# A two-layer trunk (forgetting attention, then retention) on Strassen products: the order of every engine written out in the kernel

## The chip, the cores and the metric

One core of one Trainium2 chip. The metric is device time in microseconds of one execution, the median of several. The core has TensorE (PE in the profile; its weight loads are listed apart, as PEld), VectorE (DVE), ScalarE (ACT), GpSimd (POOL) and SyncE (SP). SP issues most transfers; POOL issues those that add to what lies in memory. Each engine takes its instructions in the order of its own list, and waits on semaphores for the others.

## The reference, cut to what matters

512 tokens of width 2048, all in fp32, two layers. Every layer is one branch and one normalisation:

```python
h = layer_norm(DEEPNORM_ALPHA * h + branch(h, ...), ln_gain[i], ln_bias[i])
# layer 0, fox_branch: q, k, v, gate, f_logit = split(h @ w_in);  16 heads of 128
q, k = rms_norm(q, q_gain), rms_norm(k, k_gain)
c = cumsum(log_sigmoid(f_logit + b_f), axis=1)
s = q @ k.T * scale + c[:, None] - c[None, :]          # causal mask, softmax
branch = (softmax(s) @ v * silu(gate)) @ w_out
# layer 1, retention_branch: q, k of 8 heads of 256, v and gate of 8 heads of 512
q, k = rotary(q), rotary(k) * 256 ** -0.5
o = (q @ k.T * decay) @ v                              # given in chunks of 128, with a carried state
branch = (group_norm_heads(o) * silu(gate)) @ w_out
```

Nearly all arithmetic is in the projections: 2048 x 8192 and 2048 x 2048 in layer 0, 2048 x 12288 and 4096 x 2048 in layer 1.

## The kernel before, in words

**Products.** A projection is cut into units (class `Unit`). A unit multiplies a 2 x 2 arrangement of quarters of the activations (rows m, columns n) by a 2 x 2 arrangement of quarters of weights with seven products, p1 to p7, where the plain way has eight. The activations are prepared in seven forms (a11, s1, a12, s2, s4, s3, a22), sums and differences of their quarters that stay on chip while a layer uses them. The weights' sums are made on DVE as they stream: `operand` (L184-203) loads a block of 512 KB with `load` (L178-182), keeps a running chain tile for p1, p5, p6, p4 (L202 adds the next quarter to it) and adds two blocks for p7 (L199). Three staging tiles (ring `st`) and four chain tiles take the loads.

**Precision.** fp32 operands are split in a high and a low part (`split`, L141-144): ACT copies the high part (L143), DVE subtracts it to get the low part (L144). `mm3` (L146-150) multiplies with three matmuls: high by high, high by low, low by high.

**Blocks.** A block is 128 partitions by 1024 weights: "wide" blocks make 12 matmuls of 512 columns, "narrow" ones 24 of 256. There are 16 narrow units of 14 blocks (q and k of Fox pairs and of retention heads) and 18 wide ones of 28 (4 of Fox values and gates, 2 of the Fox output, 8 of retention values and gates, 4 of its output): 728 blocks. Each needs one ACT copy and one DVE subtraction, and 416 need a sum on DVE as well. The results of products are combined in `after` (L242-260): ACT copies p1, p5 and p6 out of their PSUM bank (`keep`, L237-239), DVE adds later products to them (L251, L255, L258), and the unit's `sink` gets each of the four result quarters.

**Everything else** stands between blocks: per Fox pair the norms (`normed`: L478 squares, L484 scales, L491 transposes, L495 splits) and two heads (`head`: L518 adds the forget bias, L523 the row extreme, L524 exp, L526 scale, L533 transposes, L534 copies, L544 products with v, L553 gate). A head's output goes to DRAM as parts of the next forms, L354 through POOL's queue where it is added to what lies there, L356 through SP's. `fetch_form` (L358-) brings forms back. After the Fox output units 4 and 5 come `add_z` (L670-685: residual and statistics), `to_columns` and `turn` (L700-720: normalise, transpose) and `combine` (L300-322: the forms of the new layer). A retention head has rotation (L771-774), scores (L789), mixing and group norm (L818-820), transposes (L832-841); its gate waits in DRAM (L607, L816). At the end `store` (L896-907) normalises with DVE, ACT (L903) and POOL (L904).

**What sets the order.** Three things. `ahead` delays each block's multiplication by two blocks behind its preparation. `pending` is a list of side steps: `tick` runs a share of it after each block, spread evenly over the blocks left in the unit, and `finish_pending` runs all that is left at the seams between layers. Above both, the framework's scheduler reorders instructions on each engine by its own estimate of when they are ready, so a line of the kernel does not show where its instruction stands.

```python
def tick():
    blocks[0] -= 1
    for _ in range(max(1, -(-len(pending) // max(blocks[0], 1)))):
        if pending:
            pending.popleft()()
```

Of the kernel before, what the change touches and what calls it, by code (L numbers as in the profile page):

```python
# [17 lines left out]
AX = mybir.AxisListType  # L18

P = 128  # L20
D = 2048
S = 512
# [23 lines left out]
def blocks_of(n, *groups):  # L46
# [9 lines left out]
HELD = ([("p1", c) for c in range(4)] + [(p, c) for p in ("p5", "p6", "p2") for c in range(3)],  # L56
        [(p, 3) for p in ("p5", "p6", "p2")] + blocks_of(4, ("p3", "p7"), ("p4",)))
# [8 lines left out]


@with_exitstack
def trunk(ctx: ExitStack, tc: tile.TileContext, xq, x, fb_f, columns, wf_in, narrow, wide, ln_g, ln_b, rot, decay,
# [4 lines left out]
    dram = ctx.enter_context(tc.tile_pool(name="dr", bufs=1, space=bass.MemoryType.DRAM))  # L74

# [8 lines left out]

    def raw8(tag):
        return pool.tile([P, 8, 256], F32, name="raw", tag=tag)

    def mmp():
        return psum.tile([P, 512], F32, name="mmp", tag="mmp", bufs=2)

    def trp():
        return mmp().rearrange("p (a b) -> p a b", a=4)
# [4 lines left out]
    make_causal_mask(nc, causal, NEG)  # L97

# [4 lines left out]

    pending = deque()
    blocks = [0]

    def tick():
        blocks[0] -= 1
        for _ in range(max(1, -(-len(pending) // max(blocks[0], 1)))):
            if pending:  # L110
                pending.popleft()()

    def finish_pending():
        while pending:
            pending.popleft()()


    ahead = deque()

    def advance(n):  # L120
        while len(ahead) > n:
            ahead.popleft()()

    def rsqrt(dst, src, n, scale, eps):

        h = pool.tile([P, n], F32, name="rsq_h", tag=f"rsq_h{n}", bufs=2 if n < 4 else 1)
        t = pool.tile([P, n], F32, name="rsq_t", tag=f"rsq_t{n}", bufs=2 if n < 4 else 1)
# [5 lines left out]
        for _ in range(3):  # L133
            if n == 1:
                nc.vector.scalar_tensor_tensor(t, dst, dst, h, op0=ALU.mult, op1=ALU.mult)
            else:
                nc.vector.tensor_mul(t, dst, dst)
                nc.vector.tensor_mul(t, t, h)
            nc.vector.scalar_tensor_tensor(dst, t, 1.5, dst, op0=ALU.subtract, op1=ALU.mult)
# [13 lines left out]
    forms = {}  # L153

    def new_form(name):
        forms[name] = [pool.tile([P, 8, 256], F32R, name=name, tag=t) for t in HOME[name]]

    def split_form(name, src, sl):
        split(src, *(t[sl] for t in forms[name]))

    chains = [0]
    pairs_of_banks = ["b0", "b1", "b2"]

    class Unit:
# [3 lines left out]
        def __init__(self, w, n, sink, rows=True):  # L168
            self.w, self.n, self.sink, self.rows = w, n, sink, rows
# [3 lines left out]
            self.keeps = {"p1": "k0", "p5": "k1", "u2": "k2"} if self.wide else {"p1": "k1", "p5": "k2", "u2": "k0"}  # L173
            self.banks = self.both = None
            self.bank, self.kept, self.chain, self.lent = {}, {}, {}, {}
            self.left = {p: self.blocks for p in FORM}

        def load(self, q, c, tag=None):  # L178
            kw = dict(tag=tag) if tag else dict(tag="st", bufs=3)
            t = pool.tile(self.shape, F32, name="w_raw", **kw)  # L180
            nc.sync.dma_start(t.rearrange("p a b -> p (a b)"), self.w[self.n, int(q[1]) - 1, int(q[0]) - 1, c])
            return t

        def operand(self, p, c, following, streamed):  # L184

            if p in ("p1", "p5") and not streamed and c not in self.chain:
                self.chain[c] = self.load("11", c, f"q{chains[0] % 4}")
                chains[0] += 1
            if p == "p1":
                return self.load("11", c) if streamed else self.chain[c]  # L190
            if p in ("p2", "p3"):
                t = self.load({"p2": "21", "p3": "22"}[p], c)
                if following == (SHARES[p], c):
                    self.lent[following] = t
                return t
            if p == "p7":
                b = self.lent.pop((p, c), None) or self.load("22", c)
                t = self.load("12", c)
                nc.vector.tensor_add(t, t, b)  # L199
                return t  # L200
            t = self.lent.pop((p, c), None) or self.load({"p5": "12", "p6": "22", "p4": "21"}[p], c)
            nc.vector.tensor_add(self.chain[c], self.chain[c], t)  # L202
            return self.chain[c]

        def accumulator(self, b):

            if self.both is None:
                if self.banks is None:
                    self.banks = dict(zip("xzy", pairs_of_banks))
                    pairs_of_banks[:] = pairs_of_banks[1:] + pairs_of_banks[:1]  # L210
                t = psum.tile([P, 2, 512], F32, name="acc", tag=self.banks[b])
                return t if self.wide else t[:, 0].rearrange("p (e n) -> p e n", e=2)
            if b == "x":
                self.pair = psum.tile([P, 2, 512], F32, name="acc", tag=self.both)
            return self.pair[:, "xzy".index(b) > 0].rearrange("p (e n) -> p e n", e=2)

        def multiply(self, p, c, w, streamed):
            a = forms[FORM[p]]
            b = BANK[p]
            new = self.left[p] == self.blocks and p in ("p1", "p2", "p5")  # L220
            if new:
                self.bank[b] = self.accumulator(b)
            self.left[p] -= 1
            n = self.shape[1]
            for k in range(n):
                for e in range(2):
                    es = slice(e * P, (e + 1) * P)
                    if self.rows:
                        l, r = [t[:, n * c + k, es] for t in a], [t[:, k] for t in w]
                    else:  # L230
                        l, r = [t[:, k, es] for t in w], [t[:, n * c + k] for t in a]
                    mm3(self.bank[b][:, e], l, r, new and k == 0 and (e == 0 or self.wide),
                        self.left[p] == 0 and k == n - 1)
            if self.left[p] == 0:
                self.after(p, streamed)

        def keep(self, what, bank):  # L237
            self.kept[what] = t = pool.tile([P, 2, self.shape[2]], F32, name=what, tag=self.keeps[what])
            nc.scalar.activation(t, self.bank[bank], AF.Copy)
# [726 lines left out]
```

## Time and profile before

| | |
|---|---|
| Median of 3 runs | 2584.55 us (2584.49 to 2587.41) |
| Profiled execution, own time | 2578.53 us |
| Its span; mean clock granted to TensorE | 2576.8 us; 0.964 |
| DMA | 507.86 MB, 197 GB/s over the span |

The span runs from the first to the last instruction of the profiled execution; the own time also holds what lies around it. In a row of a table by stretches, each engine's busy time is followed by its number of instructions; PEclk is the share of full clock that TensorE was granted there, so busy time times PEclk is the work at full clock. In the rows of groups the columns are: line, engine, operation, what it writes and reads, how often, then busy time in all, the mean of one in ns, and the idle time ahead of it with what ended it. In the rows of waits: engine, line and tile that waits, what it waits for, us in all, times, longest.

### The profile page before, as it was taken

Reading aid. Unit: us, or ns where it says so; the run is one execution under the profiler, and the core shown is the slowest. Engines: PE = TensorE matmul, PEld = TensorE weight load, DVE = VectorE, ACT = ScalarE, POOL = GpSimd, SP = SyncE. Lnnn points to the kernel's source line nnn. Section 1 sums busy time; section 2 is a strip of 40 time slices with the busy share of each in tenths; the row PEclk is TensorE's granted clock in tenths of the full one; section 3 lists DMA queues with packets and bytes.
Section 4 is the critical chain, followed back from the end, with each engine's and each line's share of the span. In section 5 each row is a group of like instructions: output and inputs, shape, how many; then the busy total and the mean of one; then the engine's idle time right before and its main releaser. Section 6 shows DMA issues by size and latency. Waiting matters only on the chain.

```text
span 2576.8 us, 34299 instructions
## 1 busy us (share of the span) xinstructions
PE 2349.0 (91%) x12820; PEld 2001.7 (78%) x12820; DVE 2004.3 (78%) x2617; ACT 1276.9 (50%) x1891; POOL 100.8 (4%) x116
## 2 busy tenths in 40 slices
PE   6899999999997898699999999999999988897994
PEld 5788898898886687579797878788888866675773
DVE  7778687777776779887878878787878788577778
ACT  5456566666566445444454444444544444343432
POOL 0000000001101000000000000000000100100001
PEclk8999999999998999899999999999999999999997
DMA  6465746645755657467566566666676666677564
GB/s 243 156 217 168 235 150 172 217 160 159 221 190 162 217 188 269 155 196 208 178 220 194 193 191 202 181 203 189 208 212 201 190 198 216 191 241 241 193 213 147
DMA packets 213159, 507.86 MB, mean 197 GB/s; under 512 B 20080, under 2 KB 76784, under 8 KB 212736
## 3 DMA queue, kind: packets, MB, share of 16 engines
q1 hardware_dynamic: 198592, 485.22, 56.9%
q0 software_dynamic: 14400, 20.45, 5.6%
q8 instruction: 100, 1.64, 0.3%
q14 instruction: 67, 0.55, 0.1%
HBM read 430.33 MB, written 75.27 MB: 196 GB/s over the span
## 4 chain that ended last, share of the span: by engine, by line
PE 24%; DVE 14%; DMA 11%; issue 4%; ACT 4%; SPq 0%; POOL 0%; ACTq 0%; POOLq 0%; DVEq 0%
PE acc L149 7%; PE acc L150 7%; PE acc L148 7%; DVE w_l L144 5%; DMA w_raw<-in_wide 4%; ACT w_h L143 3%; DVE w_raw L202 2%; DMA w_raw<-in_narrow 2%; DMA y_s<-ny 1%; DMA cos_sin<-in_rot 1%; DMA ln_g<-in_ln_g 1%; DVE w_raw L199 1%; PE mmp L148 1%; DMA gate<-rgates 1%; DMA y_raw<-y_s 1%
## 5 line engine op out<-in xcount | busy, mean ns | idle before, releaser
L143 ACT ACTIVATE w_h<-w_raw 128x1024 fp32r<-128x1024 f32 x728 | 762.7, 1057 | 919.0 <-PE acc L150 277.0
L144 DVE TENSOR_TENSOR w_l<-w_raw,w_h 128x1024 fp32r<-128x1024 f32 x728 | 882.9, 1220 | 285.5 <-ACT w_h L143 281.1
L148 PE MATMUL acc<-w_h,s 128*128 128x512 f32 (+1 forms) x1664 | 607.7, 365 | 50.6 <-ACT w_h L143 46.6
L149 PE MATMUL acc<-w_l,s 128*128 128x512 f32 (+1 forms) x1664 | 609.2, 366 | 21.2 <-DVE w_l L144 20.4
L150 PE MATMUL acc<-w_h,s 128*128 128x512 f32 (+1 forms) x1664 | 602.6, 362 | 0.0
L148 PE MATMUL acc<-w_h,a 128*128 128x512 f32 (+1 forms) x1248 | 459.8, 369 | 47.3 <-ACT w_h L143 34.6
L149 PE MATMUL acc<-w_l,a 128*128 128x512 f32 (+1 forms) x1248 | 456.4, 366 | 33.8 <-DVE w_l L144 33.8
L150 PE MATMUL acc<-w_h,a 128*128 128x512 f32 (+1 forms) x1248 | 453.6, 363 | 0.0
L202 DVE TENSOR_TENSOR w_raw<-w_raw 128x1024 f32<-128x1024 f32 x312 | 378.5, 1218 | 69.8 <-DMA w_raw<-in_narrow 34.3
L148 PEld LDWEIGHTS acc<-w_h,s 128*128 128x128 f32 x1664 | 318.7, 192 | 108.3 <-ACT w_h L143 58.5
L149 PEld LDWEIGHTS acc<-w_l,s 128*128 128x128 f32 x1664 | 319.2, 192 | 84.2 <-DVE w_l L144 40.1
L150 PEld LDWEIGHTS acc<-w_h,s 128*128 128x128 f32 x1664 | 319.2, 192 | 43.5 <-DVE s L144 0.4
L148 PEld LDWEIGHTS acc<-w_h,a 128*128 128x128 f32 x1248 | 241.7, 194 | 91.9 <-ACT w_h L143 42.4
L149 PEld LDWEIGHTS acc<-w_l,a 128*128 128x128 f32 x1248 | 241.7, 194 | 72.4 <-DVE w_l L144 38.7
L150 PEld LDWEIGHTS acc<-w_h,a 128*128 128x128 f32 x1248 | 241.5, 194 | 35.0
L199 DVE TENSOR_TENSOR w_raw<-w_raw 128x1024 f32<-128x1024 f32 x104 | 126.9, 1220 | 51.1 <-DMA w_raw<-in_wide 39.8
L148 PE MATMUL acc<-s,w_h 128*128 128x256 f32 x512 | 145.9, 285 | 5.1 <-DVE u L255 2.0
L149 PE MATMUL acc<-s,w_h 128*128 128x256 f32 x512 | 146.1, 285 | 0.0
L150 PE MATMUL acc<-s,w_l 128*128 128x256 f32 x512 | 146.0, 285 | 0.0
L148 PE MATMUL acc<-a,w_h 128*128 128x256 f32 x384 | 110.8, 288 | 1.0 <-DVE p L258 1.0
L149 PE MATMUL acc<-a,w_h 128*128 128x256 f32 x384 | 110.1, 287 | 0.0
L150 PE MATMUL acc<-a,w_l 128*128 128x256 f32 x384 | 109.9, 286 | 0.0
(187 smaller groups left out, 2558.3 us busy)
## 6 DMA issues: line engine op xcount, KB each, us to landing
w_raw<-in_wide SPq DMA_DIRECT2D x468, 512.0 KB, 4.0
w_raw<-in_narrow SPq DMA_DIRECT2D x200, 512.0 KB, 3.6
y_raw<-y_s SPq DMA_DIRECT2D x35, 256.0 KB, 4.1
gate<-rgates SPq DMA_DIRECT2D x32, 256.0 KB, 4.6
y_s<-ny POOLq DMA_DIRECT2D x32, 256.0 KB, 7.5
y_raw<-y_a SPq DMA_DIRECT2D x26, 256.0 KB, 4.0
y_a<-y SPq DMA_DIRECT2D x24, 256.0 KB, 3.0
y_s<-y POOLq DMA_DIRECT2D x24, 256.0 KB, 7.0
```

Of the source, the lines that this page charges most:

```text
L143: nc.scalar.activation(h, src, AF.Copy)
L144: nc.vector.tensor_sub(l, src, f32(h))
L148: nc.tensor.matmul(ps, a[0], b[0], start=start, stop=False, skip_group_check=True)
L149: nc.tensor.matmul(ps, a[0], b[1], start=False, stop=False, skip_group_check=True)
L150: nc.tensor.matmul(ps, a[1], b[0], start=False, stop=stop, skip_group_check=True)
L199: nc.vector.tensor_add(t, t, b)
L202: nc.vector.tensor_add(self.chain[c], self.chain[c], t)
```

## The change

The kernel switches the framework's scheduler off (`tc.manual_schedule()`): every engine runs its instructions as the program's text issues them. A class `Order` does the ordering while the program is written. Blocks stand in one line across all units; `slot` issues what belongs to block i: results of block i - 1, sums of weights up to block i + 3, splits up to block i + 2, loads up to i + 8 as tiles come free, then the matmuls of block i, then one `step` of each waiting task. Tasks (norms, heads, fetched forms, normalisation) are generators that yield `need(...)`: the estimated DVE, ACT and PE time of their next step, slots to wait, a condition, and tiles that must be free, which `Order` counts itself. A step is passed over while DVE or ACT has a debt of over 5 us by these estimates. Where a block's form or bank isn't there, `require` makes turns without a block: all tasks go on, step by step. I call these forced turns.

```diff
+    def slot(self):
+        i, n = self.at, len(self.line)
+        self.turn()
+        self.debt = [max(0.0, d - self.time) for d in self.debt]
+        self.time = 2.8
+        if i:
+            self.finish(self.line[i - 1])
+        while self.added <= min(i + 3, n - 1):
...
+            while self.split < self.added:
+                self.split_one()
+            self.debt[0] += self.line[self.added].add()
+            self.added += 1
+        while self.split <= min(i + 2, n - 1):
+            self.split_one()
+        while self.loaded < min(i + 9, n) and all(self.free[r] >= k for r, k in self.line[self.loaded].rings().items()):
+            self.line[self.loaded].load()
+            self.loaded += 1
+        b = self.line[i]
+        self.require(b.ready)
+        b.multiply()
+        self.step()
+        self.at += 1
```

```diff
+    def require(self, met):
+        for _ in range(400):
+            if met():
+                return
+            self.turn()
+            self.debt = [max(0.0, d - 2.7) for d in self.debt]
+            self.step(True)
```

Other edits that come with it:

- Writes to DRAM move from SP's queue to POOL's: the parts of the forms (`give_forms`), values and gates, normalised rows, residuals. POOL issues 258 transfers where it issued 100; SP issues fewer.
- In the two units whose order is EARLY (the last of each layer's output), the weights' sums for p7 and p4 are made by transfers that add, 16 in all, and p4 gets a bank of its own, so that its result needs a second addition in `add_z`. The order HELD of the first Fox output unit puts p7 behind p3 block by block and one block of p2 behind both.
- Retention gates stay on chip. Statistics are finished for two row tiles at once, and half of the first normalisation runs on ACT.
- The first blocks' x is loaded and split in smaller parts. Retention's first blocks are the wide ones.
- At the end DVE does all of the normalisation; ACT's scaling and POOL's additions go.
- Heads 12 and 13 of the Fox layer go through DRAM (`late_parts`): their part of the forms s1, s2, a12, s4 and a22 is fetched while the output projection has begun.

```diff
+                nc.gpsimd.dma_start(d, self.source("22", 2 * i + c), accum_op=ALU.add)
...
-            if c % 2:
-                nc.scalar.activation(z, z, AF.Copy, scale=r)
-                nc.gpsimd.tensor_add(z, z, gb[1][:, cs])
-            else:
-                nc.vector.scalar_tensor_tensor(z, z, r, gb[1][:, cs], op0=ALU.mult, op1=ALU.add)
...
+                nc.vector.scalar_tensor_tensor(z, z, r[:, e:e + 1], gb[1][:, cs], op0=ALU.mult, op1=ALU.add)
```

Counted over the program, PE keeps its 12758 instructions; DVE goes from 2619 to 2586, ACT from 1701 to 1708. The changed order has 120 forced turns: 15 around blocks 13 to 21, 49 at the first Fox output unit (blocks 224 to 238), 34 at the second seam (blocks 260 to 301), 12 around the first retention output unit, the rest at the end; none in the stretches between.

Two places show what moves. The first is ACT at the start of the first Fox output unit, while the last heads' softmax runs: L143 is the split of weights, L518, L524, L526 and L534 the steps of heads named above. Before:

```order
L143 ACTIVATE w_h_6409<-w_raw_6407 128x1024
L524 ACTIVATE p_6333,sm_6334<-p_6333,sm_6334 128x512
L524 ACTIVATE p_6363,sm_6364<-p_6363,sm_6364 128x384
L526 ACTIVATE p_6333<-p_6333,sm_6334 128x512
L143 ACTIVATE w_h_6445<-w_raw_6442 128x1024
L526 ACTIVATE p_6363<-p_6363,sm_6364 128x384
L534 ACTIVATE pT_6388<-mmp_6389 128x4x128
L518 ACTIVATE mmp_6395<-mmp_6395,c_tok_692 128x256
L534 ACTIVATE pT_6388<-mmp_6425 128x3x128
L524 ACTIVATE p_6401,sm_6402<-p_6401,sm_6402 128x256
L143 ACTIVATE w_h_6471<-w_raw_6469 128x1024
```

And with the change, where L845 is the bias, L838 exp, L834 the scale, L828 the copies and L255 the split of forms and weights alike:

```order
L834 ACTIVATE p_8158<-p_8158,sm_8161 128x512
L838 ACTIVATE p_8169,sm_8172<-p_8169,sm_8172 128x384
L845 ACTIVATE mmp_8174<-mmp_8174,c_tok_1515 128x256
L845 ACTIVATE mmp_8174<-mmp_8174,c_tok_1515 128x128
L834 ACTIVATE p_8169<-p_8169,sm_8172 128x384
L838 ACTIVATE p_8186,sm_8189<-p_8186,sm_8189 128x256
L838 ACTIVATE p_8186,sm_8193<-p_8186,sm_8193 128x128
L828 ACTIVATE pT_8207<-mmp_8202 128x4x128
L834 ACTIVATE p_8186<-p_8186,sm_8189 128x256
L834 ACTIVATE p_8186<-p_8186,sm_8193 128x128
L255 ACTIVATE s1_7938<-y_raw_8181 128x512
L255 ACTIVATE w_h_8231<-w_q_7535 128x1024
```

Before, three to five steps of heads stand between two splits of weights. Now 28 rows of ACT stand between the splits for blocks 232 and 233, and the last of them splits what heads 12 and 13 wrote to DRAM.

The second place is DVE in retention head 1: L144 is the split, L202 the sum of weights, L818 to L820 the group norm. Before:

```order
L144 TENSOR_TENSOR w_l_12062<-w_raw_12059,w_h_12061 128x1024
L818 BN_STATS gn_st_12097<-mmp_12090 128x6
L202 TENSOR_TENSOR w_raw_12059<-w_raw_12059,w_raw_12101 128x1024
L819 BN_AGGR gn_mv_12094<-gn_st_12097 128x2
L202 TENSOR_TENSOR w_raw_12010<-w_raw_12010,w_raw_12146 128x1024
L144 TENSOR_TENSOR w_l_12105<-w_raw_12059,w_h_12104 128x1024
L820 SCALAR_TENSOR_TENSOR gate_12095<-mmp_12090,gn_mv_12094,gate_12095 128x512
L818 BN_STATS gn_st_12142<-mmp_12133 128x6
L144 TENSOR_TENSOR w_l_12150<-w_raw_12010,w_h_12149 128x1024
L819 BN_AGGR gn_mv_12094<-gn_st_12142 128x2
L202 TENSOR_TENSOR w_raw_12059<-w_raw_12059,w_raw_12197 128x1024
```

With the change L256 is the split, L447 the sum, L1324 to L1326 the group norm, and L1379 a step of the residual for the next layer:

```order
L256 TENSOR_TENSOR w_l_12069<-w_raw_11935,w_h_12068 128x1024
L447 TENSOR_TENSOR w_raw_11969<-w_raw_11969,w_raw_11935 128x1024
L1379 SCALAR_TENSOR_TENSOR z_in_11924<-ln_b_11926,z_in_11924 128x512
L256 TENSOR_TENSOR w_l_12102<-w_raw_11969,w_h_12101 128x1024
L1324 BN_STATS gn_st_12132<-mmp_12032 128x6
L1325 BN_AGGR gn_mv_12131<-gn_st_12132 128x2
L1326 SCALAR_TENSOR_TENSOR p1_11432<-mmp_12032,gn_mv_12131,p1_11432 128x512
L256 TENSOR_TENSOR w_l_12146<-w_raw_12004,w_h_12145 128x1024
L447 TENSOR_TENSOR w_raw_12073<-w_raw_12073,w_raw_12004 128x1024
L1324 BN_STATS gn_st_12178<-mmp_12136 128x6
L1325 BN_AGGR gn_mv_12131<-gn_st_12178 128x2
L1326 SCALAR_TENSOR_TENSOR p1_11432<-mmp_12136,gn_mv_12131,p1_11432 128x512
```

Now each block has its split and at most one sum, and one short step of a task behind them, always in this order.

More of the change, by code (lines that the diff above doesn't have):

```diff
@@ L184, in operand, with source @@
[L184 to L203, printed above, removed]
+        def source(self, q, c):
+            return self.w[self.n, int(q[1]) - 1, int(q[0]) - 1, c]
@@ L215, in accumulator @@
[L215 to L235, printed above, removed]
@@ L282, in run @@
[L282 to L292 removed]
+                shares = i + 1 < len(order) and order[i + 1] == (SHARES.get(p), c)
+                shared = i > 0 and order[i - 1] == ({"p7": "p3", "p4": "p2"}.get(p), c)
+                o.push(Block(self, p, c, shares, shared, streamed, then.get(i), then.get(p), before.get(i)))
```

1408 lines of the change are left out of this document (956 added, 452 removed).

## Prediction

> **What bounds the kernel now.** I read the page's busy times first, then a table of nine stretches of the span, then the pitch of single matmuls, then the waits by engine.
>
> ```profile
> span 2576.8 us, 34299 instructions
> PE 2349.0 (91%) x12820; PEld 2001.7 (78%) x12820; DVE 2004.3 (78%) x2617; ACT 1276.9 (50%) x1891; POOL 100.8 (4%) x116
> ```
>
> TensorE is the busiest, but 91% is an average, and part of it is work at a low clock. The stretches are (1) the first two units, (2) six Fox pairs, (3) the first and (4) the second Fox output unit, (5) the second normalisation with retention head 0, (6) heads 1 to 6, (7) head 7 with the first retention output unit, (8) the last three units, (9) the tail.
>
> ```profile
> core 0: us, PE busy (x) PEld busy (x) DVE busy (x) ACT busy (x) POOL busy (x), PEclk, DMA share, GB/s
> 0.00:169.00 169.00, 141.04 (x794) 121.13 (x795) 130.66 (x160) 86.11 (x127) 1.09 (x8) 0.96 0.60 208
> 169.00:787.50 618.50, 608.32 (x3913) 541.57 (x3913) 469.66 (x701) 395.38 (x793) 35.21 (x40) 1.00 0.61 185
> 787.50:908.20 120.70, 101.72 (x437) 78.43 (x436) 91.23 (x147) 67.89 (x143) 3.47 (x4) 0.90 0.65 199
> 908.20:1003.10 94.90, 86.75 (x370) 69.48 (x370) 77.03 (x107) 41.11 (x53) 0.00 (x0) 0.95 0.67 221
> 1003.10:1166.70 163.60, 135.24 (x733) 115.60 (x732) 137.46 (x166) 75.14 (x91) 0.00 (x0) 0.92 0.57 190
> 1166.70:2003.80 837.10, 799.81 (x4450) 690.62 (x4449) 668.10 (x833) 382.33 (x445) 34.78 (x40) 0.99 0.65 198
> 2003.80:2272.50 268.70, 230.49 (x1125) 190.11 (x1125) 197.31 (x248) 115.65 (x131) 13.95 (x16) 0.94 0.68 206
> 2272.50:2555.90 283.40, 245.57 (x1009) 194.77 (x1008) 218.01 (x225) 110.60 (x109) 6.07 (x4) 0.93 0.63 209
> 2555.90:2576.80 20.90, 0.01 (x1) 0.00 (x0) 14.79 (x36) 2.67 (x4) 6.24 (x4) 0.62 0.26 101
> ```
>
> PE busy times the granted clock is the work at full clock: 135.4, 608.3, 91.5, 82.4, 124.4, 791.8, 216.7, 228.4 and 0. It sums to 2279; the span holds 298 us beside it. The losses by stretch are 33.6, 10.2, 29.2, 12.5, 39.2, 45.3, 52.0, 55.0 and 20.9. So stretch 2 is nearly full, and the loss lies at the seams and in retention. DVE's share, over stretches 1 to 8, is 73 to 84%: busy, not full.
>
> What a block costs TensorE is read from the distance between matmuls, wide blocks first, then narrow:
>
> ```profile
> 1849.80 0.39 PE L149 MATMUL acc<-w_l,a 128*128 128x512 f32 x1
> ...
> 1855.92 0.39 PE L149 MATMUL acc<-w_l,a 128*128 128x512 f32 x1
> 319.73 0.28 PE L149 MATMUL acc<-w_l,a 128*128 128x256 f32 x1
> ...
> 320.93 0.28 PE L150 MATMUL acc<-w_h,a 128*128 128x256 f32 x1
> ```
>
> The first two lie 27 matmuls apart, 0.2267 us each: 12 make a wide block of 2.72 us. The others lie 10 apart, 0.12 each: 24 make a narrow block of 2.88.
>
> What TensorE waits for (us in all, times, longest), and what ACT's weight copies wait for:
>
> ```profile
> PE acc L148 <- ACT w_h L143: 81.2, 46, 8.7
> PE acc L149 <- DVE w_l L144: 54.1, 41, 15.6
> PE mmp L835 <- ACT gate L832: 21.2, 12, 4.4
> ```
> ```profile
> ACT w_h L143 <- DVE w_raw L202: 272.9, 94, 8.8
> ACT w_h L143 <- DVE w_raw L199: 155.7, 50, 9.5
> ```
>
> TensorE waits for weights that are split too late: 135 us of its waits are for their high or low half. The copy is late since the sum on DVE ahead of it was late. That is a matter of place in DVE's and ACT's orders, which the change sets, not of their rates:
>
> ```profile
> L143 ACT ACTIVATE w_h<-w_raw 128x1024 fp32r<-128x1024 f32 x728 | 762.7, 1057 | 919.0 <-PE acc L150 277.0
> L144 DVE TENSOR_TENSOR w_l<-w_raw,w_h 128x1024 fp32r<-128x1024 f32 x728 | 882.9, 1220 | 285.5 <-ACT w_h L143 281.1
> L202 DVE TENSOR_TENSOR w_raw<-w_raw 128x1024 f32<-128x1024 f32 x312 | 378.5, 1218 | 69.8 <-DMA w_raw<-in_narrow 34.3
> ```
>
> A block needs 1.22 us of DVE for the split and, in 4 of 7 products, 1.22 for a sum: at most 2.44 of 2.72, so steps of about 1 us a block fit on the average.
>
> Such waits also cost clock:
>
> ```profile
> 2543.14 0.47 PE L148 MATMUL acc<-w_h,a 128*128 128x512 f32 x1 [2.14 <-ACT w_h L143]
> ...
> 2543.91 0.57 PE L148 MATMUL acc<-w_h,a 128*128 128x512 f32 x1
> 2544.28 0.63 PE L149 MATMUL acc<-w_l,a 128*128 128x512 f32 x1
> 2544.71 0.63 PE L150 MATMUL acc<-w_h,a 128*128 128x512 f32 x1
> ...
> 2547.27 0.45 PE L150 MATMUL acc<-w_h,a 128*128 128x512 f32 x1
> ```
>
> After 2.14 us of idle the pitch is 0.43, half speed, for 3.4 us, which adds about 1.6 us. Over the stretches busy time times (1 - clock) makes 70 of the 298 us. The Trainium skill ("TensorE: Matmul & The Clock Gate", Part 1) says the gate falls to half only after an idle window of about 3.4 us. The idle row here is shorter and half speed followed, so the measurement decides. By the page's rule the short stalls left below would cost no clock, and the sum would be about 30 us lower: 5 us of clock in each of the six stretches that I leave with losses.
>
> **The change part by part.** TensorE's work is the same 12758 instructions, so 2279 us stays. What moves is where DVE and ACT work stands. Weights are summed three blocks and split two blocks ahead, always, and one short step of each task follows a block. In the steady stretches the order has no forced turn (a place where several steps run with no block between): I let the losses fall there to what fixed distances can't cover.
>
> Stretch 2: 608.3, less one pair's attention that slips behind the seam. Its small matmuls are costed from two pairs:
>
> ```profile
> 312.40:499.80 187.40, 185.63 (x1173) 163.92 (x1172) 143.39 (x217) 120.28 (x247) 6.12 (x7) 1.00 0.57 180
> ```
>
> 28 narrow and 28 wide blocks take 156.8 of 185.6, so a pair's small matmuls take 14.4; ACT has 120.3 less 56 splits of 1.057, 30.5 a pair. With 3 of loss: 608.3 - 14.4 + 3 = 597.
>
> Stretch 3 turns worse. Blocks 224 to 239 now hold the heads of two pairs, 1.8 pairs of steps, in 49 forced turns. Here ACT fills first: 16 splits make 17, 1.8 pairs at 27 (30.5 without the results kept) make 48, late forms some 13: about 78 to 80 against 16 blocks of 2.72 = 43.5. Then block 230 can't begin before heads 12 and 13 were written to DRAM and read back:
>
> ```profile
> y_raw<-y_s SPq DMA_DIRECT2D x35, 256.0 KB, 4.1
> y_s<-ny POOLq DMA_DIRECT2D x32, 256.0 KB, 7.5
> y_a<-y SPq DMA_DIRECT2D x24, 256.0 KB, 3.0
> ```
>
> A write on POOL's queue (7.5), a read on SP's (4.1), and splits behind both are 15 to 25: I take 20. With 80 + 20, twelve further blocks at 2.72 (33) and 5 for the clock, 138 against 120.7: the seam loses 17 us.
>
> Stretch 1: a lead-in, then DVE's combination of x. The first matmul now:
>
> ```profile
> 8.20 0.58 PE L148 MATMUL acc<-w_h,a 128*128 128x256 f32 x1 [8.20 <-ACT w_h L143]
> ```
>
> Loading x in smaller pieces makes that 7. Between the splits of blocks 10 and 24 DVE has 45 operations of 1.22 and small ones, 56 us, against 39.7 of PE work, less the 5.6 that splits run ahead: 11. 135.4 + 7 + 11 = 153.
>
> Stretch 4: sixteen sums in all become accumulating DMAs (two units of eight; 19.5 us of DVE). Reads are unchanged in bytes, and the DMA share of 0.67 covers them; if it didn't, 7.5 us would show once per product. 82.4 + 1 = 83; at the old loss 95.
>
> Stretch 5: 33 forced turns. Between blocks 278 and 301 DVE's instructions, at the durations of the rows above, make about 86 us against 73 for 24 blocks and the small matmuls: 13, plus 7 for the chain of normalisation and transposes and 5 of clock: 124.4 + 25 = 150.
>
> Stretches 6, 7, 8: losses fall to a third: 791.8 + 15 = 807, 216.7 + 18 = 235 (12 forced turns), 228.4 + 15 = 243. From no loss to the old one they lie between 1237 and 1389. I take the lower third because stretch 2, where the same splits run beside heavier ACT work, already loses 1.7% against 5.7, 24 and 24% of the work here: the split rate is no limit.
>
> Tail: no matmul; the rows that matter, beside POOL's work and alone:
>
> ```profile
> L906 DVE SCALAR_TENSOR_TENSOR z<-z,ln_r,ln_last 128x512 f32<-128x512 f32 x8 | 8.7, 1125 | 0.0
> L820 DVE SCALAR_TENSOR_TENSOR gate<-mmp,gn_mv,gate 128x512 f32<-128x512 f32 x32 | 23.9, 748 | 8.2 <-DMA gate<-rgates 7.8
> ```
>
> DVE takes over ACT's and POOL's part, 4 to 6 operations more, but each at about 0.75 in place of 1.125: 22 (18 to 26).
>
> Writes that stood between the weight loads on SP's queue now stand on POOL's, 258 issues for 100:
>
> ```profile
> L354 POOL DMA_DIRECT2D y_s<-ny x58 | 54.4, 1063 | 604.3 <-ACT qk_raw L467 199.5 <-DMA y_s<-ny 190.9 <-ACT ny L841 72.8
> ```
>
> At 1.06 us that is 273 us of POOL, 11% of the span, off the path except at the seam. SP gains nothing on the path while the loads run up to nine blocks ahead.
>
> Sum: 153 + 597 + 138 + 83 + 150 + 807 + 235 + 243 + 22 = 2428. The profiled execution took 2578.53 by its own time, 1.73 over its span; the median of the runs, 2584.55, is 6.02 more. So 2430 of own time, and 2436 as median.
>
> Edits with one answer, taken at nothing: the retention gates stay on chip (fewer DMAs, under shares of 0.57 to 0.68), statistics are finished for two row tiles at once, half of the first normalisation goes to ACT, which is busy 75 of 164 us in stretch 5. What hides them is TensorE's blocks; without that cover none is worth over 5 us.
>
> **The rivals.** *Leaner seams* (0.20). A forced turn may cost only its busiest engine, and the steady losses may all but vanish. For it: DVE is below 85% in every stretch. Against: 120 forced turns. Halving my 149 us of loss gives about 2365. The floor is 2279 of work, 7 of lead-in, 22 of tail and 8: 2316.
>
> *Heavier seams* (0.12). A forced turn is a round trip between engines that no block hides. One such step:
>
> ```profile
> L478 ACT ACTIVATE mmp<-qk_raw 128x128 f32<-128x128 f32 x128 | 33.8, 264 | 0.5
> L478 ACT ACTIVATION_READ_ACCUMULATOR mmp<-qk_raw 128x1 f32 x128 | 24.1, 188 | 0.0
> ```
>
> Four of each make 1.8 us; with the hand-over to the next engine I take 1.9. At that, stretch 3 holds 93 + 43.5 + 20 + 33 + 5 = 195 and stretch 5 124 + 63 = 187 and 10 for the rest: with some 15 at the start and in stretch 7, 120 us more, 2556. For it: the seam loses 29.2 us in 28 blocks already, ten times what stretch 2 loses per block.
>
> *POOL's queue* (0.05). Twelve writes of heads 12 and 13 and eight of the normalised rows stand in one line at 1.06, and two landings of 7.5 show: 36 us, 2472. The Trainium skill ("SBUF — State Buffer", Who interferes with whom) has GpSimd's DMAs starved while DVE holds the shared ports, which would make this dearer. With DVE 78% busy the L354 row still shows 1.06 us an issue; that L906 is slow beside POOL agrees with the page's lock.
>
> *Blocked in order* (0.11, slower). Each engine now waits at the head of a written order: a weight split on ACT stands behind a kept result or a step that waits for TensorE, and a scheduler no longer puts ready work first. The place is ACT's and DVE's order in the steady stretches, with some 670 blocks. It decides from 148/670 = 0.22 us a block; one DVE operation of 1.22 in every fourth block is 0.305 and 204 us: 2640. Against: splits two blocks ahead leave 5.4 us, and a step is held back once either engine owes 5 us. For: DVE's 78% leaves little to catch up with.
>
> *No change* (0.04, 2580 to 2590): the order before may already have been near this one, its losses being chains. Against: the waits for w_h and w_l come from sums that stand late.
>
> **How the numbers follow.** The forecast, 2436, has 0.48, its own range 2390 to 2490. The range over all cases is 2350 to 2590: it leaves out a quarter of the lean case, the slower rival and little else. About 0.2% is what a measurement of this kernel tells from no change. Faster: 0.48 + 0.20 + 0.05 + 0.11 of the heavier seams = 0.84; within 0.2%: 0.04; slower: the blocked order and the last 0.01, 0.12.
>
> **What would show it.** Work at full clock stays 2279. Right: stretch 6 within 800 to 820, waits of TensorE for w_h and w_l under 50 us in all, the Fox output seam longer than 120.7, with ACT the releaser, DVE's sums ahead of the copies by a block. Wrong: waits spread thinly over all steady blocks (blocked order), a seam stretch above 190 (heavier) or POOL transfers as releasers of SP's reads for more than 30 us.

## The result, and the profile after

The changed kernel takes 2813.62 us (median of four runs, 2807.18 to 2818.12) where the kernel before takes 2585.98: the ratio is 1.0873, interval 1.0843 to 1.0902. It is 8.7% slower; the forecast was 2436, 6% faster.

The first lines of the page:

```profile
span 2812.5 us, 34239 instructions
...
PE 2421.5 (86%) x12820; PEld 2044.4 (73%) x12820; DVE 2015.2 (72%) x2584; ACT 1280.6 (46%) x1898; POOL 190.8 (7%) x284
```

DVE and ACT are busy for nearly as long as before (2004.3 and 1276.9 us), so the loss is not added work of theirs. The table by stretches, cut at the same blocks as the one in the prediction:

```profile
core 0: us, PE busy (x) PEld busy (x) DVE busy (x) ACT busy (x) POOL busy (x), PEclk, DMA share, GB/s
0.00:219.40 219.40, 154.78 (x769) 132.64 (x770) 121.20 (x122) 79.25 (x111) 2.87 (x11) 0.84 0.43 150
219.40:890.70 671.30, 619.12 (x3873) 548.11 (x3872) 473.73 (x699) 378.99 (x754) 62.74 (x93) 0.97 0.53 166
890.70:1089.20 198.50, 135.47 (x503) 101.73 (x502) 101.61 (x176) 91.51 (x191) 9.21 (x12) 0.74 0.42 128
1089.20:1191.80 102.60, 83.76 (x353) 66.44 (x352) 75.43 (x102) 38.91 (x42) 9.13 (x12) 0.93 0.70 218
1191.80:1426.70 234.90, 162.63 (x746) 134.25 (x745) 132.78 (x150) 82.70 (x112) 2.14 (x4) 0.81 0.34 115
1426.70:2247.80 821.10, 795.49 (x4453) 682.08 (x4452) 681.46 (x838) 384.94 (x452) 68.78 (x101) 1.00 0.63 190
2247.80:2511.30 263.50, 230.78 (x1125) 189.47 (x1125) 201.23 (x249) 117.70 (x135) 22.45 (x31) 0.95 0.66 198
2511.30:2783.00 271.70, 239.49 (x1009) 189.67 (x1007) 202.67 (x207) 106.56 (x106) 13.43 (x20) 0.96 0.68 214
2783.00:2812.50 29.50, 0.00 (x0) 0.00 (x0) 25.07 (x48) 0.00 (x0) 0.00 (x0) 0.53 0.34 130
```

Busy time times clock is 2285 us, as before (2279). The rest is idle time of TensorE (2812.5 - 2421.5 = 391 us, before 228) and a low clock (136 us, before 70). Against before the length changes by +50, +53, +78, +8, +71, -16, -5, -12 and +9 us: lost at the two seams, at the start and in the Fox pairs, a little won in retention.

What TensorE waits for has changed in kind. Its two longest rows now are:

```profile
PE acc L260 <- ACT s L255: 92.3, 18, 12.6
PE acc L260 <- ACT w_h L255: 47.4, 12, 17.4
```

Over all such rows it waits 83.7 us for high and low parts of weights, where it waited 135.3 before, and 141.8 us for forms (tiles `s` and `a`), for which the kernel before has no row. So TensorE now stands more at forms that come late than at weights.

Two rows of the other engines show why they come late, DVE's wait for ACT's high part and ACT's for DVE's sum:

```profile
DVE w_l L256 <- ACT w_h L255: 585.1, 426, 6.6
ACT w_h L255 <- DVE w_q L451: 531.9, 225, 23.0
```

The same row of the kernel before:

```profile
DVE w_l L144 <- ACT w_h L143: 281.1, 247, 4.1
```

DVE stands 304 us longer at a low part whose high part isn't there. Such idle time costs nothing by itself; it costs where TensorE needs what stands behind it. What that looks like, two blocks of the second seam, in order of time (start, length, engine; in brackets the idle time before and what ended it):

```profile
1266.98 1.06 ACT L255 ACTIVATE w_h<-w_q 128x1024 fp32r<-128x1024 f32 x1 [5.86 <-PE acc L261]
1268.07 1.23 DVE L256 TENSOR_TENSOR w_l<-w_q,w_h 128x1024 fp32r<-128x1024 f32 x1 [5.69 <-ACT w_h L255]
1269.21 1.22 DVE L545 TENSOR_TENSOR raw<-raw 128x1024 f32<-128x1024 f32 x1
1270.46 1.06 ACT L255 ACTIVATE s<-raw 128x1024 fp32r<-128x1024 f32 x1 [2.43 <-DVE raw L545]
1271.57 0.58 PE L260 MATMUL acc<-s,w_h 128*128 128x256 f32 x1 [4.57 <-ACT s L255]
...
1277.37 0.60 ACT L339 ACTIVATE p<-acc 128x512 f32<-128x512 f32 x1 [5.85 <-PE acc L262]
1277.86 1.05 ACT L255 ACTIVATE w_h<-w_raw 128x1024 fp32r<-128x1024 f32 x1
1278.94 1.23 DVE L256 TENSOR_TENSOR w_l<-w_raw,w_h 128x1024 fp32r<-128x1024 f32 x1 [6.16 <-ACT w_h L255]
1280.08 1.22 DVE L447 TENSOR_TENSOR w_raw<-w_raw 128x1024 f32<-128x1024 f32 x1
1281.22 1.22 DVE L552 TENSOR_TENSOR raw<-raw 128x1024 f32<-128x1024 f32 x1
1282.47 1.06 ACT L255 ACTIVATE s<-raw 128x1024 fp32r<-128x1024 f32 x1 [3.56 <-DVE raw L552]
1283.58 0.58 PE L260 MATMUL acc<-s,w_h 128*128 128x256 f32 x1 [6.25 <-ACT s L255]
```

While TensorE works on the block ahead of the first excerpt, ACT stands at the copy of a weight for a later block, which waits 5.86 us until TensorE leaves one of three buffers. In the second it stands 5.85 us at L339, the copy of a result that TensorE hasn't finished, and the weight's copy stands behind that. In DVE's order come the low part of the weight, then in the second case a sum (L447), then the step (L545, L552) that makes the form which the very next block needs. So DVE and ACT idle while TensorE works, and TensorE idles (4.57 and 6.25 us) while they work.

### The profile page after: what moved, and what is told of

It is laid out like the page before. It is cut to its first block, busy times and chain, and to the rows that moved or that the text cites. A ratio compares the mean times of both kernels' runs of the same rounds, so it can differ in the third digit from the quotient of the medians.

```text
span 2812.5 us, 34239 instructions
## 1 busy us (share of the span) xinstructions
PE 2421.5 (86%) x12820; PEld 2044.4 (73%) x12820; DVE 2015.2 (72%) x2584; ACT 1280.6 (46%) x1898; POOL 190.8 (7%) x284
## 5 line engine op out<-in xcount | busy, mean ns | idle before, releaser
L255 ACT ACTIVATE w_h<-w_q 128x1024 fp32r<-128x1024 f32 x408 | 429.9, 1058 | 770.4 <-DVE w_q L451 531.9
L256 DVE TENSOR_TENSOR w_l<-w_q,w_h 128x1024 fp32r<-128x1024 f32 x408 | 497.9, 1223 | 334.7 <-ACT w_h L255 331.5
L260 PE MATMUL acc<-w_h,s 128*128 128x512 f32 (+1 forms) x1664 | 619.9, 373 | 98.3 <-ACT s L255 60.8
L262 PE MATMUL acc<-w_h,s 128*128 128x512 f32 (+1 forms) x1664 | 609.7, 366 | 9.5 <-DVE s L256 9.4
L256 DVE TENSOR_TENSOR w_l<-w_raw,w_h 128x1024 fp32r<-128x1024 f32 x312 | 380.3, 1223 | 255.0 <-ACT w_h L255 253.1
L260 PE MATMUL acc<-w_h,a 128*128 128x512 f32 (+1 forms) x1248 | 466.8, 374 | 63.4 <-ACT w_h L255 21.2
L255 ACT ACTIVATE w_h<-w_raw 128x1024 fp32r<-128x1024 f32 x312 | 326.3, 1054 | 372.2 <-DVE w_raw L447 192.9
L262 PE MATMUL acc<-w_h,a 128*128 128x512 f32 (+1 forms) x1248 | 459.9, 369 | 5.0 <-DVE a L256 5.0
L260 PEld LDWEIGHTS acc<-w_h,s 128*128 128x128 f32 x1664 | 326.3, 196 | 159.2 <-ACT s L255 65.3
L451 DVE TENSOR_TENSOR w_q<-w_q,w_raw 128x1024 f32<-128x1024 f32 x304 | 371.2, 1221 | 26.1 <-DMA w_raw<-in_wide 23.1
L262 PEld LDWEIGHTS acc<-w_h,s 128*128 128x128 f32 x1664 | 325.0, 195 | 58.4 <-DVE s L256 14.2
L447 DVE TENSOR_TENSOR w_raw<-w_raw 128x1024 f32<-128x1024 f32 x96 | 117.0, 1219 | 23.9 <-DMA w_raw<-in_wide 23.9
L260 PEld LDWEIGHTS acc<-s,w_h 128*128 128x128 f32 x512 | 103.8, 203 | 34.2 <-ACT s L255 33.0
```

The costliest lines, as they stand in the source:

```text
L255: nc.scalar.activation(h, src, AF.Copy)
L256: nc.vector.tensor_sub(l, src, f32(h))
L260: nc.tensor.matmul(ps, a[0], b[0], start=start, stop=False, skip_group_check=True)
L262: nc.tensor.matmul(ps, a[1], b[0], start=False, stop=stop, skip_group_check=True)
L447: nc.vector.tensor_add(self.t, self.t, u.lent.pop(("p3", c)))
L451: nc.vector.tensor_add(u.chain[c], u.chain[c], t)
```

## The experiments

All start from the changed kernel unless said. Each is a single run but for the last, on one of several chips; the kernel before took 2573 to 2583 us beside them, and its seven runs on one chip lie between 2567.78 and 2583.87. So I read a difference under some 15 us only where stretches or several runs agree on it. "Free order" means that the scheduler orders the engines.

**Forced turns ahead of the slot's splits.**

```diff
             self.finish(self.line[i - 1])
+        b = self.line[i]
+        if i > 3:
+            self.require(b.ready)
         while self.added <= min(i + 3, n - 1):
...
-        b = self.line[i]
         self.require(b.ready)
```

> The changed kernel (2813.6 us) with one thing moved: the forced turns of a slot are issued ahead of that slot's weight sums and splits instead of behind them; the work is the same. Theory A (a form's split stands on ACT and DVE behind a weight split that must wait until the block before has left one of three buffers, so ACT idles while TensorE works and TensorE idles while ACT works): blocks 280 to 322 fall from 235 us to under 190, blocks 0 to 42 from 219 to under 190, in all 80 to 120 us less, about 2710. Theory B (a forced turn is a round trip between engines wherever it stands): within 20 us of 2814.

Measured: 2718.56, 95 us less. Its first and fifth stretch:

```profile
0.00:182.20 182.20, 146.11 (x769) 124.93 (x770) 120.88 (x122) 79.08 (x111) 2.87 (x11) 0.92 0.51 181
...
1136.70:1326.70 190.00, 150.95 (x747) 124.78 (x746) 133.56 (x149) 83.45 (x113) 2.14 (x4) 0.87 0.41 146
```

Stretch 5 fell from 234.9 to 190.0, stretch 1 from 219.4 to 182.2. The same forced turns cost less in another place, so theory B falls as the whole cause and the time is the one that theory A gave. That the wait for a buffer is what makes the place dear is read from the excerpt above. The Fox pairs didn't change (671 and 673), and stretch 3 fell only from 198.5 to 182.2; the free order, next, needs 152.7 for stretch 5 and 139.2 for stretch 3, so the place is not all of the loss at the seams.

**The scheduler free.**

```diff
-    ctx.enter_context(tc.manual_schedule())
```

> The changed kernel with only the line that fixes the order taken out, so that the framework's scheduler moves the same instructions. If the written order is what costs (theory A, or waiting in order in general): 2540 to 2620 us, the seams back to their length before. If what the text brings costs (more writes on POOL's queue, weight sums by transfer, heads 12 and 13 through DRAM, the end on DVE alone): still over 2740.

Measured: 2475.62, 338 us under the changed kernel and 101 under the kernel before on the same chip (2576.24). The text gains; the written order costs more than three times that. Its stretches:

```profile
0.00:154.90 154.90, 137.67 (x777) 119.28 (x778) 126.95 (x148) 80.40 (x113) 2.88 (x11) 0.97 0.62 221
154.90:754.40 599.50, 594.49 (x3865) 535.45 (x3864) 460.16 (x677) 378.14 (x754) 62.75 (x93) 1.00 0.59 187
754.40:893.60 139.20, 118.78 (x503) 89.21 (x502) 97.67 (x175) 87.14 (x188) 9.22 (x12) 0.91 0.57 173
893.60:988.00 94.40, 81.21 (x350) 65.17 (x349) 70.92 (x97) 38.05 (x40) 9.29 (x12) 0.96 0.82 254
988.00:1140.70 152.70, 135.31 (x749) 116.93 (x750) 132.25 (x156) 85.48 (x117) 2.14 (x4) 0.94 0.49 170
1140.70:1932.00 791.30, 781.68 (x4454) 686.55 (x4453) 672.62 (x838) 386.67 (x450) 69.03 (x102) 1.00 0.63 198
```

And the two waits:

```profile
DVE w_l L256 <- ACT w_h L255: 249.3, 237, 5.3
ACT w_h L255 <- DVE w_q L451: 222.8, 80, 21.6
```

Both are more than halved. Counted in DVE's order: in the changed kernel all 400 sums stand right behind the split of the block before, with no split between a sum and its own block's. With the scheduler 264 of the 400 stand one to five splits further ahead.

**Two steps a block before the seam**, with turns_first:

```diff
         b.multiply()
         self.step()
+        if 196 <= i < 238:
+            self.turn()
+            self.step()
```

> The kernel turns_first, and tasks make two steps a block instead of one in blocks 196 to 237, so that heads 12 and 13 end before the first Fox output unit. If the two pairs of heads at that seam are a cost of their own: blocks 210 to 252 fall from 244 us (181 before the change) to about 200, some 30 to 45 us less than turns_first in all. If the seam is only theory A: within 10 us of turns_first.

Measured: 2700.84, 18 us less than turns_first, all of it in blocks 224 to 252 (182.2 to 162.5). The second pair's heads are a cost of their own there, about half of what was expected.

**EARLY sums on DVE**, from a second load in place of the transfer that adds:

```diff
-            self.sums = u.early and p in ("p7", "p4")
+            self.sums = False
+            self.two = u.early and p == "p7"
...
```

> The changed kernel with the sixteen weight sums of the two EARLY units made on DVE again, from two loads, instead of by transfers that add on POOL's queue. Theory C (the burst of transfers in the last unit holds a weight load back; TensorE waits 17.4 us there once): 10 to 25 us less, about 2795, with that wait gone. Theory D (DVE has no room there): 10 to 20 us more.

Measured: 2818.99, no gain. The wait in the last unit is gone and blocks 700 to 728 are 10.7 us shorter, but blocks 252 to 280 are 16.8 longer, with 13.3 us more of DVE, and the tail is 7.6 longer. Both theories were right, each in one unit.

**Splits behind the steps**, with turns_first: in `slot` the sums and splits move behind `self.step()`.

```diff
-        while self.added <= min(i + 3, n - 1):
...
         b.multiply()
         self.step()
+        if i > 3:
+            self.prepare(i, n)
```

> The kernel turns_first (2718.6 us), and in each slot the weight sums and splits are issued behind the slot's matmuls and steps instead of ahead of them, so no step stands behind a split that waits for a block to end. If theory A holds in the steady stretches too: blocks 42 to 224 fall from 673 us to under 640, in all 2640 to 2690. Theory E (there TensorE waits in its own order, since a step's matmuls stand right behind the copies that feed them): blocks 42 to 224 stay within 15 us of 673, or grow since splits start later.

Measured: 2713.16, nearly nothing: the Fox pairs gained 19 us, which lies between the two forecasts, and heads 1 to 6 lost 26. That is no place for all splits, and theory A is not shown for the steady stretches by it.

**A gap behind the norms**, with turns_first:

```diff
             give("in1")
+            yield need()
             fox["norms"] = self.i + 1
```

> The kernel turns_first, and a pair's first scores are put one slot behind the last step of its norms instead of into the same pass. Theory E: the six waits of TensorE for the copies of the normed q and k (16.9 us) go, and the clock lost behind each, 15 to 30 us less, about 2695. Theory A for the steady stretches: no change within 8 us, since another wait takes their place.

Measured: 2691.22, 27 us less, 23.5 of it in blocks 42 to 224. TensorE's waits in the Fox pairs of turns_first had begun with this row, which is gone from them here:

```profile
PE mmp L262 <- ACT qk_h L776: 16.9, 6, 3.4
```

Six waits that sum to 16.9 us cost 23.5: TensorE's idle time in these blocks fell by 13.0 us, some of it going to other waits, and the same matmuls were busy 10.5 us less, at a granted clock of 0.99 against 0.97. Theory E holds for them.

**Writes back on SP, sums back on DVE, both under the free order.** The edits are `nc.gpsimd.dma_start` to `nc.sync.dma_start` for writes that don't add, and that of sums_dve.

> The kernel sched (2475.6 us) with all plain writes to DRAM issued on SP's queue again, only those that add left on POOL's. If the move of the writes is part of what the text gains: 10 to 30 us more. If it is nothing on the path: within 6 us of 2476.

> The kernel sched with the sixteen sums of the EARLY units on DVE again. In the written order that was worth nothing (2819.0 against 2813.6). If the sums by transfer are part of what the text gains, once the order is free: 10 to 20 us more, in blocks 252 to 280 and 700 to 728. Else within 6 us of 2476.

Measured: 2461.49 and 2473.29. The two kernels with these writes on POOL's queue took 2473 and 2476, this one and the four runs of the last experiment, with the writes on SP's, 2452 to 2461: the queue costs some 14 us, opposite to what was expected. The sums by transfer are worth nothing that these runs can tell.

**The written order kept for some engines only**, the scheduler ordering the others:

```diff
-    ctx.enter_context(tc.manual_schedule())
+    ctx.enter_context(tc.manual_schedule(engines={mybir.EngineType.DVE}))
```

> The changed kernel with the written order kept for TensorE alone; the scheduler orders the other engines (sched, all free: 2475.6 us; all fixed: 2813.6). Theory E (TensorE waiting in its own order) as the larger part of what is left beside theory A's 95 us: 2550 to 2650. If the harm is on ACT and DVE: under 2510.

> The written order kept for ACT alone. Theory A (steps on ACT stand behind a weight split that waits for a buffer): 2560 to 2680. If DVE's order or TensorE's is needed for the harm: under 2510.

> The written order kept for DVE alone. Theory A by way of DVE (the low part stands behind the high part of ACT, and steps and sums behind both): 2540 to 2650. If ACT's order alone carries theory A: under 2510.

> The written order kept for every engine but TensorE. If TensorE's order adds theory E's part: 60 to 120 us under 2813.6. If TensorE must wait anyhow since the others come late: within 20 us of it.

Measured: 2519.08, 2566.29, 2694.62 and 2744.13. Over the free order TensorE's order costs 43 us, ACT's 91, DVE's 219; all but TensorE's 269, and TensorE's comes on top with 69. So the order of DVE is the larger harm, where I had looked at ACT first. Cut at the same blocks, stretches 1 and 5 take 219 and 215 us with DVE's order alone, 190 and 198 with ACT's, and 157 and 157 with TensorE's, which is near the free order's 155 and 153. The Fox pairs take 618, 598 and 620 us (free 600): the loss there comes with DVE's and TensorE's. DVE's wait with its order alone kept:

```profile
DVE w_l L256 <- ACT w_h L255: 468.0, 347, 6.4
```

**Sums ahead of the split of the block before**, alone and with turns_first:

```diff
-            while self.split < self.added:
+            x = self.line[self.added]
+            while any(y.u is x.u and y.c == x.c and not y.shares for y in self.line[self.split:self.added]):
                 self.split_one()
-            self.debt[0] += self.line[self.added].add()
+            self.debt[0] += x.add()
...
```

> The changed kernel, all orders written, with each block's weight sum issued ahead of the split of the block before it where that block does not read the same chain tile (303 of 400 sums; in the changed kernel all 400 stand right behind that split). Theory F (on DVE a sum stands behind a low part, which waits for ACT's high part, which waits for a buffer that TensorE holds, so DVE and ACT wait for one another in turn): DVE's wait for w_h falls from 585 us to under 450, and 60 to 150 us go, about 2710. If the sums' place is nothing and only the tasks' steps behind splits matter: within 15 us of 2814.

> The same with the forced turns ahead of the splits as in turns_first (2718.6 us). If theories A and F are two costs: 60 us or more under the better of the two, 2600 to 2650. If they are one and the same wait: within 20 us of the better of the two.

Measured: 2723.82 and 2622.85. Alone 90 us less, with turns_first 191 less: the two add up and are two costs. The edit's other lines only count when a staging tile comes free. DVE's wait falls to 382.0 and, with both, to 275.5, near the free order's 249.3:

```profile
DVE w_l L257 <- ACT w_h L256: 382.0, 291, 6.3
```
```profile
DVE w_l L259 <- ACT w_h L258: 275.5, 274, 6.0
```

**All four moves in the written order**, and then the low parts later still (a subtraction is issued behind the slot's step; in lows_late the low parts of p6 in the two EARLY units are taken from a tile to which the next sum was already added, so it computes something else and its time is not read; lows_behind takes them ahead of that sum):

> All orders written, with the four moves of the single runs together: sums ahead of splits (-90), forced turns ahead of splits (-95; both together -191), the gap behind the norms (-27) and two steps a block at the seam (-18). If they add up: 2570 to 2585 us, level with the kernel before. If the last two are covered by the first two: 2610 to 2625.

> The kernel four_moves, and the subtraction that makes a weight's low part is issued behind the slot's step instead of right behind ACT's high part, so that DVE does the step while ACT waits for a buffer. If DVE standing at the low part is what is left of the cost: 30 to 80 us less than four_moves, under 2550. If what is left is elsewhere (ACT's and TensorE's order): within 15 us, or more, since low parts come later.

> The kernel four_moves (2593.8 us) with the low part of every weight issued behind the slot's step, as in lows_late, but tiles are given free, and the EARLY sums are added, only behind the low part, and loads are tried again behind it. If lows_late was slow (2658.6) because low parts come too late for their block: again 2630 to 2670. If it was slow because of its tiles and sums: at or under 2594.

Measured: 2593.78, 2658.58 and 2613.34. The four moves take 220 of the 338 us, 10 less than their sum of 230, and bring the kernel within 0.5% of the one before. Later low parts don't help. In lows_behind DVE's wait for the high part falls from 259.4 to 160.4 us and the time doesn't fall with it, so that wait is not what is left of the cost: theory F ends with the sums.

**The version that the runs point to**: the changed text, free order, plain writes on SP, sums on DVE.

> The changed text with the scheduler free, plain writes on SP's queue and the EARLY sums on DVE. The single effects were 14.1 and 2.3 us under 2475.6: if they add up, 2455 to 2463; in any case 4 to 5% under the kernel before.

Measured: 2458.21, median of four (2451.71 to 2460.70), ratio to the kernel before 0.9547, interval 0.952 to 0.9574: 4.5% faster than before, 12.6% under the changed kernel (2813.62).

```profile
PE 2318.3 (95%) x12820; PEld 1995.5 (81%) x12820; DVE 1995.7 (81%) x2600; ACT 1281.0 (52%) x1898; POOL 88.1 (4%) x108
```

## Why the prediction was wrong

**The step that failed** is "In the steady stretches the order has no forced turn ...: I let the losses fall there to what fixed distances can't cover", and its like at the seams, where the length was taken from the busiest engine's rate. Both price an order by rates, as if each engine could take what is ready. The sum has no term for an instruction that waits and holds back all that stands behind it. With the scheduler free the stretches come near the forecast; with the written order they don't:

| stretch | forecast | free order (sched) | changed kernel |
|---|---|---|---|
| 1, first two units | 153 | 154.9 | 219.4 |
| 2, Fox pairs | 597 | 599.5 | 671.3 |
| 3, first output unit | 138 | 139.2 | 198.5 |
| 4, second output unit | 83 | 94.4 | 102.6 |
| 5, second seam, head 0 | 150 | 152.7 | 234.9 |
| 6, heads 1 to 6 | 807 | 791.3 | 821.1 |
| 7, head 7, first output unit | 235 | 251.4 | 263.5 |
| 8, last units | 243 | 267.9 | 271.7 |
| 9, tail | 22 | 22.6 | 29.5 |

The free order does not keep the forced turns and fixed distances that the forecast priced. That it comes within 3 us of the forecast in stretches 1, 3 and 5 is luck as far as the runs tell, and confirms none of those terms.

**The wait that was to shrink** did: 83.7 us of TensorE's waits are for high or low parts, against 135.3, though not under the 50 that was named. What the forecast lacked is a term for the forms, whose splits stand in the same two lists: 141.8 us.

**Work at full clock** stayed, as said. **The 2.44 of 2.72 us a block** was true as a rate and hid the chain: in the written order a block's sum waits for a low part, that for a high part, that for a buffer. The rows to see it were there. The second excerpt of the order shows L256 directly ahead of L447, and I read it as "one short step" a block. The description of `slot` at the start, sums three blocks ahead and splits two, is true of its numbers, and yet in DVE's list each sum stands right behind the split of the block before, and can't run before that split's buffer is free.

**Seams.** The 49 and 34 forced turns were rightly named as the danger. Heavier seams gave 195 for stretch 3, and it took 198.5, over the 190 that was named as its sign; in stretch 5 it gave 187 and the kernel took 234.9. Its reason, that a turn is a round trip wherever it stands, is not the whole: with the turns ahead of the splits stretch 5 took 190.0 and stretch 3 182.2. What is left of the two against the free order (37 and 43 us) may hold round trips; of it four_moves takes 16 and 25 by sums, gap and steps, and no run parts the rest. That a seam already loses "ten times" what stretch 2 loses per block is too little: 29.2 us in 28 blocks against 10.2 in 182 is nearly nineteen times. The excerpt of ACT's order at this seam told less than it seemed to: the profile has 33 rows, not 28, between those two splits, and the kernel before has 30 between two splits five blocks earlier.

**Blocked in order** was the right rival with the wrong place. It put the loss thinly over all steady blocks; heads 1 to 6 became 16 us shorter. Against the free order, though, the written one costs 30 us there and 72 in the Fox pairs, so 102 of the 338 us do lie in the steady stretches, partly hidden by what the text gains. The larger part lies where a step's result is needed by the next block (seams, start). Its chance of 0.11 leaned on "splits two blocks ahead leave 5.4 us", which holds only if nothing that the next block needs stands behind them.

**Tail.** 29.5 against 22. The longer operations did get shorter, 752 ns against 1125 beside POOL's work, as argued:

```profile
L1433 DVE SCALAR_TENSOR_TENSOR z<-z,ln_r,ln_last 128x512 f32<-128x512 f32 x16 | 12.0, 752 | 0.6
```

but DVE is busy 25.1 us in the tail of the written order and 19.3 in that of the free one, which did more of these operations before the last matmul. With DVE's order alone kept the tail takes 29.4, with ACT's or TensorE's alone 22.6: it is DVE's order again.

**POOL's queue** costs some 14 us under the free order, where the rival had 36, and not at the seams where the rival looked: stretches 3 and 5 of sched and sched_sp differ by 1 us. POOL issues 276 transfers in the changed kernel, 16 of them sums, and not 258. The sums by transfer, priced as a gain of DVE time, gave none. In the last unit a load comes late beside them; DVE's sum waits for it, and TensorE behind that (without these sums the wait is gone, as sums_dve shows):

```profile
2736.57 1.23 DVE L451 TENSOR_TENSOR w_q<-w_q,w_raw 128x1024 f32<-128x1024 f32 x1 [20.18 <-DMA w_raw<-in_wide]
```
```profile
2739.03 0.80 PE L260 MATMUL acc<-w_h,s 128*128 128x512 f32 x1 [17.44 <-ACT w_h L255]
```

**The clock.** The prediction speaks of 5 us of clock in each of six stretches, but only stretches 3 and 5 have such a term in the sum. The low clock took 136 us, against 70 before.

**Still open.** The last 118 us between four_moves (2593.78) and sched. Some 86 of them lie in stretches 1, 2, 3 and 5 and 26 in heads 1 to 6; fix_act and fix_pe show that ACT's and TensorE's orders have a share, not which rows. Nor do the runs tell which part of the text gains the 101 us under the free order; 63 of them lie in stretches 6 and 7 (837.1 + 268.7 against 791.3 + 251.4).

## What to carry to other kernels

A written order is not priced by each engine's busy time per block: for every instruction that can wait, list what stands behind it on its engine, and ask whether someone waits for that. A wait for a buffer that the busiest engine holds was dear in front here, so put sums and steps for the next block ahead of splits for later ones. Keeping the order of one engine at a time and freeing the rest tells in one run each which list carries the harm. A wait of an engine that isn't the busiest is a clue and not a price: look for what the busiest engine waits for behind it.

## What the runs showed of the hardware

The harm is that of lists taken strictly from the front. The Trainium skill ("PSUM — Partial Sum Buffer", Engine vs sequencer instructions) says that the queues of ScalarE and VectorE are strict FIFO; the trace agrees, with DVE idle 6.16 us at L256 while a sum and a step stood behind it, and sums_ahead shows what the sums' place alone is worth.

Waits cost clock too, short ones among them. In the Fox pairs of turns_first no wait of TensorE was longer than 3.4 us, and taking six of them away (gap) raised the granted clock from 0.97 to 0.99. In stretch 3 of the changed kernel, with waits of up to 12.6 us, it was 0.74. Over the kernel the low clock took 136 us beside 391 of idle time: about a third on top.
